# Output projection of a hybrid decoder layer: three pairs of row blocks by Strassen's algorithm

## The chip, the cores and the metric

The kernel runs on one core of a Trainium2 chip. The metric is device time in microseconds (us) of one launch. PE is the matrix engine, DVE the vector engine, ACT the scalar engine, POOL the GpSimd engine; SP is the engine that only issues transfers (the sync queue). ACT issues transfers too (its own queue), between its instructions.

## The reference

One decoder layer over 512 tokens of width 1024, in fp32. Cut to what matters here:

```python
mod = silu(c) @ ada_w + ada_b                     # adaLN: 48 blocks of 128 values
sh1, sc1, g1, sh2, sc2, g2 = split(mod, 6)
...
h = mlstm(...)                                    # 4 heads x 256 = 1024 columns
y = silu(layer_norm(causal_dwconv(a * sigmoid(gt)))) # 1024 columns
mix = concatenate([h, y]) @ w_out                 # (512 x 2048) @ (2048 x 1024)
x = x + g1 * rms_norm(mix, mix_post_g)
u = rms_norm(x, ffn_pre_g) * (1.0 + sc2) + sh2
up = causal_dwconv(u @ ffn_up)                    # then gated, ffn_down, second residual
```

## The kernel before

Every fp32 product is made of three passes: both operands are split into a high part that the matrix engine takes exactly (`hi`, a copy on ACT) and a low part (`lo`, a subtraction), and `mm3` adds hi x hi, hi x lo and lo x hi into one PSUM bank. Weights are split by `w_split`: the high part on ACT, the low part on POOL. The split blocks live in a ring of 20 tiles, ten blocks of 128 rows x 512 columns (`wpool`); raw weights come in 1 MB pieces through two buffers (`raws`) on the sync queue.

The output projection multiplies 16 row blocks of `w_out` (128 rows each: 0 to 7 from the four heads, 8 to 15 from the convolution) by the tokens, in four tiles of 128 tokens. It makes the first half of the 1024 columns (`mixa`, four PSUM banks) and then the second (`mixb`, four banks). `MIX` is the order of the blocks: those of the last head (6, 7) come late, since this head's attention is still running. `mix_first(n)` is the n-th block of the first half; calls of it stand between the steps of the last head's attention, so that PE always has something to do. The attention ends with eight transposes (`hT`); ten blocks of the first half stand ahead of them on PE, six behind. Then follow eight blocks of the second half (`KA = 8`), over all four banks. The last eight blocks are done one token tile at a time (`mix_last`), so that the norm, the residual and the modulation of a token tile (`chain_sums`, `chain_x`, `chain_u`) run beside the next tile's matmuls.

Between `KA` blocks and `mix_last` PE transposes the rows of gains for the FFN (`send_rows(KT, 2 * KT)`, tile `gT`), which go to DRAM and come back spread over all partitions (`gs2r`, `sh2r`). These gains need adaLN blocks 24 to 39. An adaLN block (`ada_block`, L147 to L157) fetches 512 KB on ACT's queue and sums it on DVE in one instruction with two inputs in SBUF; it is ordered on DVE behind the instruction that it is given. The sixteen blocks stand behind the last head's attention, and have six buffers, four of them in a tile `spare`. ACT's queue also fetches the residual `x` (eight pieces of 256 KB) and the spread row `g1r`.

The orders of PE and of the sync queue are the program's. A scheduler orders ACT, DVE and POOL by priority (program order, with `tc.cur_priority` and added dependencies as exceptions) and by when it expects operands. The FFN's down projection already works by Strassen's algorithm in Winograd's form (`forms`, `prod1`, `prod2`).

Of the kernel before, what the change touches and what calls it, by code (L numbers as in the profile page):

```python
# [22 lines left out]
H = 4  # L23
# [24 lines left out]

MIX = [*range(6), *range(8, 14), 6, 7, 14, 15]


@with_exitstack
def decoder_layer(ctx, tc, w_glu0, x, xT, c, adaT, vecs, w_glu, w_qko, w_v0, w_v, w_out, w_up, w_down, out):
    nc = tc.nc
# [92 lines left out]
    def ada_block(i, behind):  # L147

        if i % 6 < 4 and 24 <= i < 40:
            r = spare[0][:, 2 * (i % 6) : 2 * (i % 6) + 2, :].rearrange("p j t -> p (j t)")  # L150
        else:
            r = adas.tile([P, D], F32, tag="ada", name=f"ada_{i}")
        nc.scalar.dma_start(r, adaT[i // 2][:, (i % 2) * D : (i % 2 + 1) * D])
        junk = small.tile([P, D], BF16, tag="junk", bufs=1, name=f"junk_{i}")
        t = V.scalar_tensor_tensor(out=junk, in0=r, scalar=1.0, in1=cb, op0=ALU.mult, op1=ALU.mult, accum_out=mod[:, i : i + 1])  # L155
        tc.add_manual_dep(t.ins, behind.ins.name, mybir.DependencyInfo(mybir.DependencyClass.NoSync, mybir.DependencyReason.DATA),
                          reason="order on VectorE")  # L157
# [27 lines left out]

    def mm3(ps, a, b, start, stop):

        PE.matmul(ps, a[0], b[0], start=start, stop=False)  # L188
        PE.matmul(ps, a[0], b[1], start=False, stop=False)  # L189
        PE.matmul(ps, a[1], b[0], start=False, stop=stop)  # L190

# [249 lines left out]
    def pair(z, hi, lo):  # L441
        S.activation(hi, z, AF.Copy)
        V.tensor_tensor(out=lo, in0=z, in1=hi.bitcast(F32), op=ALU.subtract)
        return hi, lo

    def conv4(ps, i, name):
# [43 lines left out]
    def attention(h):  # L490
# [50 lines left out]
        for e in range(2):  # L541
# [4 lines left out]
            t = so[e]  # L546
            V.scalar_tensor_tensor(out=t, in0=t, scalar=1.0, in1=tp, op0=ALU.add, op1=ALU.mult)
            hi, lo = slot(f"hh{h}_{e}", F32R), slot(f"hl{h}_{e}", F32R)
            g = ghalf[:, 2 * h + e : 2 * h + e + 1]
# [89 lines left out]

    def send_rows(a, n, queue=nc.scalar):  # L640

        ps = mmbank(f"gT{a}") if a == KT else atbank(f"gT{a}")
        PE.transpose(ps[:n, :P], gains[:, a : a + n], ident)
        t = slot(f"gTs{a}")[:, :P]
        V.tensor_copy(t[:n, :], ps[:n, :P])
        for i in range(n // KT):
            queue.dma_start(rows_d[a // KT + i].rearrange("(j p) -> j p", p=P), t[i * KT : (i + 1) * KT, :])
# [38 lines left out]
    def wo_rows(hf, g):  # L686
        return w_load(w_out[hf, g], f"wo{hf}_{g}")

    mixa = [mmbank(f"mixa{tt}") for tt in range(NT)]

    def mix_first(n):
        if n % 4 == 0:
            wo[0] = wo_rows(0, n // 4)
        k = MIX[n]
        for tt, ps in enumerate(mixa):
            mm3(ps, (hy[k][0][:, tok(tt)], hy[k][1][:, tok(tt)]), wo[0][n % 4], n == 0, n == 2 * KT - 1)

# [64 lines left out]
    def norm_rows():  # L762
        yb = rms_bcast(yr[0], T, 1.0 / D, "ry", cvbank)
        for j in range(KT):
            V.tensor_tensor(out=ys[j], in0=ys[j], in1=yb, op=ALU.mult)
            S.activation(ys[j], ys[j], AF.Silu, bias=vcol("cv_ln_b", j), scale=vcol("cv_ln_g", j))
            hi, lo = slot(f"yh{j}", F32R), slot(f"yl{j}", F32R)
# [40 lines left out]
    gain(0, 16, "mix_post_g")  # L808
    wo = {}
    steps = attention(H - 1)  # L810
    next(steps)
    mix_first(0)
    next(steps)
    norm_rows()
    mix_first(1)
    mix_first(2)
    mix_first(3)
    mix_first(4)
    next(steps)
# [3 lines left out]
    next(steps)  # L823
    for n in range(7, 10):
        mix_first(n)
    for _ in steps:
# [5 lines left out]
    for n in range(10, 2 * KT):  # L832
        mix_first(n)
        if n == 10:
            send_rows(0, KT)
    mg = [slot(f"mg{tt}") for tt in range(NT)]
    x1 = [[slot(f"x1_{tt}_{hf}") for hf in range(2)] for tt in range(NT)]
    wide1 = vpool.tile([P, 2 * T + 8], F32, tag="vh", name="g1r")
    g1r = row(0, lambda n: [wide1[:, :T], wide1[:, T : 2 * T]], "g1")
    for tt in range(NT):  # L840
        for hf in range(2):
            nc.scalar.dma_start(x1[tt][hf], x[tok(tt), hf * T : (hf + 1) * T])
    for tt, ps in enumerate(mixa):
        V.tensor_tensor(out=mg[tt], in0=ps, in1=g1r[0], op=ALU.mult)
        sq_sum(ps, msq[:, 2 * tt : 2 * tt + 1], f"mixa{tt}")
    banks = [atbank(f"mixb{tt}") if tt < 2 else cvbank(f"mixb{tt}") for tt in range(NT)]
    for n_, k in enumerate(MIX[:KA]):
        if n_ % 4 == 0:
            wo = wo_rows(1, n_ // 4)
        for tt, ps in enumerate(banks):  # L850
            mm3(ps, (hy[k][0][:, tok(tt)], hy[k][1][:, tok(tt)]), wo[n_ % 4], n_ == 0, False)
    V.scalar_tensor_tensor(out=gains[:, KT : 2 * KT], in0=sc2[:, :, 0], scalar=1.0, in1=vcols("ffn_pre_g", 0, KT), op0=ALU.add, op1=ALU.mult)
    V.tensor_scalar(out=gains[:, KT : 2 * KT], in0=gains[:, KT : 2 * KT], scalar1=RD, scalar2=None, op0=ALU.mult)
    V.tensor_copy(gains[:, 2 * KT : 3 * KT], sc2[:, :, 1])
    wo = [w for g in range(KA // 4, 4) for w in wo_rows(1, g)]

    HT = T // 2
    u2h = upool.tile([P, 2, KT, HT], F32R, tag="uh", name="u2h")
# [43 lines left out]
    def mix_last(tt, a, b):  # L902
        for n_, k in enumerate(MIX[KA:]):
            if a <= n_ < b:
                mm3(banks[tt], (hy[k][0][:, tok(tt)], hy[k][1][:, tok(tt)]), wo[n_], False, n_ == 2 * KT - KA - 1)

# [27 lines left out]
    with in_order():  # L934
        for tt in range(3):
            mix_last(tt, 0, 2 * KT - KA)
        up_split(1, raw1, slots, "t")
# [11 lines left out]
        turn_tile(1)  # L949
        mix_last(3, 7, 2 * KT - KA)  # L950
        r = chain_sums(2)
# [309 lines left out]
def _layout(i):  # L1261
# [9 lines left out]
    def tiles(w, starts, per):  # L1271
# [20 lines left out]
    a0 = 4 * D + 2 * H  # L1292
    wo = f("w_out")[0]
    return {
        "w_glu0": c_(np.stack([cols(w_in, a0 + b * D + j * P) for j in range(4) for b in range(2)]).transpose(2, 1, 0, 3).reshape(KT, P, 8 * P)),
# [8 lines left out]
        "w_v": c_(np.stack([vw(w_in[:, 2 * D + h * DH : 2 * D + (h + 1) * DH]) for h in range(1, H)])),  # L1304
        "w_out": c_(wo.reshape(2 * KT, P, 2, T)[MIX].reshape(4, NT, P, 2, T).transpose(3, 0, 2, 1, 4).reshape(2, 4, P, 4 * T)),
        "w_up": tiles(f("ffn_up")[0], [b * DFF + j * P for j in range(NF) for b in range(2)], 2),
# [21 lines left out]
```

## Time and profile before

| | us |
|---|---|
| median of 3 runs | 773.85 |
| lowest, highest | 772.72, 775.44 |
| profiled execution, its own time | 772.58 |
| profiled execution, span of instructions | 770.9 |
| PE busy in the span | 757.8 |
| DVE, ACT, POOL busy in the span | 606.3, 403.9, 350.9 |

Rows in order of time read: start in us, duration in us, engine, line of the kernel, operation, out<-in, tile sizes, count, and in brackets the engine's idle time just before and what ended it. Durations of matmuls overlap (the next starts before the last ends), so the pitch is taken from starts.

### The profile page before, as it was taken

The page shows a single profiled execution, that of the slowest core. Times are in us where ns is not written, and L with a number is a line of the kernel's source. Part 1 is how long each engine was busy: PE and PEld are TensorE (multiplying, and loading weights), DVE is VectorE, ACT ScalarE, POOL GpSimd, SP SyncE. Part 2 cuts the span into 40 slices and gives each one's busy share as a digit, 9 for nine tenths or more (in the row PEclk, how much of TensorE's full clock was granted, in tenths as well). Part 3 has the DMA queues.
Part 4 walks back from the last instruction along what each step waited for, and adds up shares of the span by engine and source line. Part 5 has one row for each costly group of instructions (what it writes and reads, how often), then busy time and mean ns, then how long its engine had stood idle before and what let it go on. Part 6 is the DMA issues. An engine that isn't in the chain of part 4 may idle for free.

```text
span 770.9 us, 10631 instructions
## 1 busy us (share of the span) xinstructions
PE 757.8 (98%) x3709; PEld 637.3 (83%) x3709; DVE 606.3 (79%) x967; ACT 403.9 (52%) x761; POOL 350.9 (46%) x286
## 2 busy tenths in 40 slices
PE   7999999999999999999999999999999999999996
PEld 5788898778888888988888998888888888878885
DVE  6987999999999856747758798666555687699996
ACT  5447256677676457572343554444444444455762
POOL 1029578697797645442751456444444440000001
PEclk9999999999999999999999999999999999999998
DMA  8983214204023552425953653333233321787872
GB/s 325 341 334 137 84 55 164 82 29 164 28 82 110 166 177 96 162 111 187 379 195 114 245 187 130 130 130 109 96 117 124 131 91 60 260 277 226 302 261 109
DMA packets 36409, 125.33 MB, mean 163 GB/s; under 512 B 4194, under 2 KB 5634, under 8 KB 30468
## 3 DMA queue, kind: packets, MB, share of 16 engines
q1 hardware_dynamic: 24372, 96.17, 35.5%
q10 hardware_dynamic: 11984, 28.48, 10.6%
q8 instruction: 29, 0.48, 0.2%
q14 instruction: 24, 0.20, 0.1%
HBM read 113.22 MB, written 11.42 MB: 162 GB/s over the span
## 4 chain that ended last, share of the span: by engine, by line
PE 90%; DVE 4%; DMA 2%; ACT 2%; issue 1%; POOL 0%; SPq 0%; DVEq 0%; ACTq 0%; POOLq 0%
PE up L190 10%; PE up L189 10%; PE up L188 10%; PE qko L188 6%; PE qko L189 5%; PE qko L190 5%; PE p L1175 5%; PE glu L189 3%; PE glu L188 3%; PE glu L190 3%; PE glu L316 2%; PE mixa L190 2%; PE mixa L188 2%; PE mixa L189 2%; PE mixb L188 2%; PE mixb L190 2%
## 5 line engine op out<-in xcount | busy, mean ns | idle before, releaser
L721 DVE SCALAR_TENSOR_TENSOR cv<-gt,cvw,cv 128x489 f32<-128x489 f32 (+23 forms) x200 | 136.9, 728 | 3.3 <-ACT cv L709 2.2
L675 POOL TENSOR_TENSOR ro2r<-ro2t,mhalf 128x1 f32<-128x1 f32 x1 | 0.5, 537 | 120.5 <-DVE ro2t L673 120.5
L171 POOL TENSOR_TENSOR wup_1024l<-wup,wup_1024h 128x512 fp32r<-128x512 f32 x20 | 27.5, 1373 | 31.7 <-ACT wup_1024h L170 31.6
L717 POOL TENSOR_TENSOR cs<-cs,cs 128x510 f32<-128x510 f32 (+3 forms) x32 | 41.3, 1291 | 0.2
L171 POOL TENSOR_TENSOR wup_0l<-wup,wup_0h 128x512 fp32r<-128x512 f32 x20 | 27.3, 1367 | 29.1 <-ACT wup_0h L170 29.1
L171 POOL TENSOR_TENSOR wup_1536l<-wup,wup_1536h 128x512 fp32r<-128x512 f32 x20 | 27.0, 1349 | 28.8 <-ACT wup_1536h L170 28.8
L155 DVE SCALAR_TENSOR_TENSOR junk<-ada,cb 128x1024 bf16<-128x1024 f32 x20 | 31.1, 1554 | 7.8 <-DMA ada<-in_adaT 7.7
L189 PE MATMUL up<-u2l,wup_0h 128*128 128x512 f32 (+1 forms) x100 | 36.5, 365 | 0.2 <-DVE u2l L900 0.2
L188 PE MATMUL up<-u2h,wup_0h 128*128 128x512 f32 (+1 forms) x100 | 36.5, 365 | 0.0
L188 PE MATMUL up<-u2h,wup_1024h 128*128 128x512 f32 (+1 forms) x100 | 36.4, 364 | 0.0
L190 PE MATMUL up<-u2h,wup_0l 128*128 128x512 f32 (+1 forms) x100 | 36.4, 364 | 0.0
L188 PE MATMUL up<-u2h,wup_512h 128*128 128x512 f32 (+1 forms) x100 | 36.4, 364 | 0.0
L189 PE MATMUL up<-u2l,wup_512h 128*128 128x512 f32 (+1 forms) x100 | 36.4, 364 | 0.0
L190 PE MATMUL up<-u2h,wup_512l 128*128 128x512 f32 (+1 forms) x100 | 36.4, 364 | 0.0
L188 PE MATMUL up<-u2h,wup_1536h 128*128 128x512 f32 (+1 forms) x100 | 36.4, 364 | 0.0
L189 PE MATMUL up<-u2l,wup_1536h 128*128 128x512 f32 (+1 forms) x100 | 36.4, 364 | 0.0
L190 PE MATMUL up<-u2h,wup_1536l 128*128 128x512 f32 (+1 forms) x100 | 36.4, 364 | 0.0
L190 PE MATMUL up<-u2h,wup_1024l 128*128 128x512 f32 (+1 forms) x100 | 36.4, 364 | 0.0
L189 PE MATMUL up<-u2l,wup_1024h 128*128 128x512 f32 (+1 forms) x100 | 36.3, 363 | 0.0
L171 POOL TENSOR_TENSOR wup_512l<-wup,wup_512h 128x512 fp32r<-128x512 f32 x20 | 27.7, 1383 | 14.9 <-ACT wup_512h L170 14.9
L715 ACT ACTIVATE cs<-gt,cvw 128x511 f32<-128x511 f32 (+4 forms) x40 | 27.4, 715 | 8.1 <-POOL cs L717 3.6
L170 ACT ACTIVATE wup_1024h<-wup 128x512 fp32r<-128x512 f32 x22 | 13.9, 631 | 25.1 <-PE up L189 21.4
(1070 smaller groups left out, 2663.6 us busy)
## 6 DMA issues: line engine op xcount, KB each, us to landing
wup<-in_w_up SPq DMA_DIRECT2D x22, 1024.0 KB, 6.6
wqko<-in_w_qko SPq DMA_DIRECT2D x12, 1024.0 KB, 4.8
ada<-in_adaT ACTq DMA_DIRECT2D x20, 512.0 KB, 4.3
ada<-in_adaT SPq DMA_DIRECT2D x16, 512.0 KB, 7.4
wo<-in_w_out SPq DMA_DIRECT2D x8, 1024.0 KB, 4.8
spare<-in_adaT ACTq DMA_DIRECT2D x12, 512.0 KB, 7.6
wd<-in_w_down SPq DMA_DIRECT2D x6, 768.0 KB, 6.5
g2kept<-g2d SPq DMA_DIRECT2D x11, 384.0 KB, 7.3
```

The source lines that it names most:

```text
L155: t = V.scalar_tensor_tensor(out=junk, in0=r, scalar=1.0, in1=cb, op0=ALU.mult, op1=ALU.mult, accum_out=mod[:, i : i + 1])
L170: S.activation(hi[:, :n], src, AF.Copy)
L171: (eng or G).tensor_tensor(out=lo[:, :n], in0=src, in1=hi[:, :n].bitcast(F32), op=ALU.subtract)
L188: PE.matmul(ps, a[0], b[0], start=start, stop=False)
L189: PE.matmul(ps, a[0], b[1], start=False, stop=False)
L190: PE.matmul(ps, a[1], b[0], start=False, stop=stop)
L316: PE.matmul(banks0[i], blk(wk, i)[a], u[k][b], start=k == 0 and a == b, stop=False)
L675: G.tensor_tensor(out=r, in0=t, in1=mhalf[:, :1], op=ALU.pow)
L715: S.activation(t[:, d:], cvx[j][:, : T - d], AF.Copy, scale=w(CK - 1 - d))
L717: G.tensor_tensor(out=side[:, d:], in0=side[:, d:], in1=t[:, d:], op=ALU.add)
L721: last_tap[0] = V.scalar_tensor_tensor(out=cp[:, d:], in0=cvx[j][:, : T - d], scalar=w(CK - 1 - d), in1=cp[:, d:], op0=ALU.mult, op1=ALU.add)
L1175: PE.matmul(ps[q], x, y, start=False, stop=m == NM - 1 and i == 2, skip_group_check=True)
```

## The change

Ten row blocks (0 to 5 and 8 to 11) stay plain in both halves. The other six form three pairs: (12, 13), (14, 15) and (6, 7). For a pair, tokens are cut into two halves of 256, columns into two halves of 512 and rows into the two blocks, and the 2 x 2 x 2 product is made from seven products instead of eight, in Winograd's form, for both column halves at once. A product is two matmul groups of 128 tokens x 512 columns.

- `token_forms` makes sums and differences of token halves on DVE and splits them; `row_forms` and `row_late` make those of the weights.
- The products are summed over the three pairs in PSUM: P2 onto the first two `mixa` banks and P4 onto the other two, P1, then P6, then P7 in two `mixb` banks, P5 and P3 in the other two. ACT copies P1, P5 and the partial sums out, and DVE adds them where they belong (`mix_done` and the additions beside it). The second half's plain blocks are then added onto the `mixb` banks; `KA` is 2.
- The raw weights of the pairs (`w_os`, 3 MB) go into tiles that take the place of the first stage's activations. The first gains' transpose stands ahead of the last head's transposes.
- AdaLN blocks 24 to 27 stand behind the first pair's token forms, 28 to 31 behind the last pair's, 32 to 35 and 36 to 39 between the products. They have four buffers.
- `x`, the first gains' row and `g1r` go through the sync queue.

```diff
-MIX = [*range(6), *range(8, 14), 6, 7, 14, 15]
+MIX = [*range(6), *range(8, 12)]
+PAIRS = [(12, 13), (14, 15), (6, 7)]
...
-        if i % 6 < 4 and 24 <= i < 40:
-            r = spare[0][:, 2 * (i % 6) : 2 * (i % 6) + 2, :].rearrange("p j t -> p (j t)")
+        if i % 4 < 2 and 24 <= i < 40:
+            r = spare[0][:, i % 4, :]
...
-    KA = 8
+    KF = 10
+    KA = 2
...
+    def token_forms(za, zb, name):
+        sums, s4 = cvtile(f"os{name}"), cvtile(f"o4{name}")
+        s1, s2 = sums[:, :HT], sums[:, HT:]
+        V.tensor_tensor(out=s1, in0=za[:, HT:], in1=zb[:, HT:], op=ALU.add)
+        V.tensor_tensor(out=za[:, HT:], in0=za[:, :HT], in1=za[:, HT:], op=ALU.subtract)
+        V.tensor_tensor(out=s2, in0=s1, in1=za[:, :HT], op=ALU.subtract)
+        V.tensor_tensor(out=s4[:, :HT], in0=zb[:, :HT], in1=s2, op=ALU.subtract)
+        a, c, b = (pair(z, slot(f"oh{name}{n}", F32R), slot(f"ol{name}{n}", F32R)) for n, z in (("a", za), ("s", sums), ("b", zb)))
+        t = slot(f"o4{name}t", F32R)
+        t = pair(s4[:, :HT], t[:, :HT], t[:, HT:])
+        last_lo[0] = last_pair[0]
...
+    def row_forms(m):
+        b21, b11, b12, b22 = (wraw[m][:, b * T : (b + 1) * T] for b in range(4))
+        wf["p1", m] = w_split(b11, f"ob1_{m}")
+        t1 = cvtile(f"ot1_{m}")
+        V.tensor_tensor(out=t1, in0=b12, in1=b11, op=ALU.subtract)
+        wf["p5", m] = w_split(t1, f"ot1_{m}")
+
+    def row_late(which, m):
+        b = {"p2": 0, "p6": 1, "p7": 2, "p3": 3, "p4": 0}[which]
+        z = wraw[m][:, b * T : (b + 1) * T]
+        if which == "p4":
+            V.tensor_tensor(out=z, in0=z, in1=wraw[m][:, T : 2 * T], op=ALU.subtract)
+        elif which == "p6":
+            t3 = wraw[m][:, 2 * T : 3 * T]
+            V.tensor_tensor(out=t3, in0=wraw[m][:, 3 * T :], in1=t3, op=ALU.subtract)
+            V.tensor_tensor(out=z, in0=z, in1=t3, op=ALU.add)
+        wf[which, m] = w_split(z, f"o{which}_{m}")
+
+    def block(which, m):
+        ps = {"p1": banks[2:], "p6": banks[2:], "p7": banks[2:], "p5": banks[:2], "p3": banks[:2], "p2": mixa[:2], "p4": mixa[2:]}[which]
+        for q in range(2):
+            mm3(ps[q], tf[m][which][q], wf[which, m], m == 0 and which in ("p1", "p5"), m == 2, True)
...
     next(steps)
     norm_rows()
+    tf[0] = token_forms(ys[4], ys[5], "0")
...
+    for i in range(24, 28):
+        ada_block(i, last_lo[0])
+    tf[1] = token_forms(ys[6], ys[7], "1")
+    for n in range(7, KF):
         mix_first(n)
+    send_rows(0, KT, nc.sync, cvbank)
...
+    for m in range(3):
+        row_forms(m)
+    for m in range(3):
+        row_late("p2", m)
     for _ in steps:
         pass
-    spare.append(upool.tile([P, KT, T], F32, tag="ul", name="spare"))
-    for i in range(24, 40):
+    tf[2] = token_forms(*heads[H - 1][3], "2")
+    for i in range(28, 32):
         ada_block(i, last_lo[0])
...
+    for which in ("p1", "p5"):
+        for m in range(2):
+            block(which, m)
+    for m in range(2):
+        block("p2", m)
+    for which in ("p1", "p5"):
+        block(which, 2)
...
+    for i in range(32, 36):
+        ada_block(i, last_lo[0])
+
+    def mix_done(tt, also):
+        V.tensor_tensor(out=mixa[tt], in0=mixa[tt], in1=also, op=ALU.add)
+        V.tensor_tensor(out=mg[tt], in0=mixa[tt], in1=g1r[0], op=ALU.mult)
+        sq_sum(mixa[tt], msq[:, 2 * tt : 2 * tt + 1], f"mixa{tt}")
+
+    for which in ("p2", "p6", "p4", "p7", "p3"):
+        for m in range(3):
+            if which != "p2":
+                row_late(which, m)
+            if which != "p2" or m == 2:
+                block(which, m)
+        if which == "p2":
+            for q in range(2):
+                mix_done(q, op1[q])
+            for i in range(36, 40):
+                ada_block(i, last_lo[0])
+        elif which == "p6":
...
+                S.activation(ou[q], banks[2 + q], AF.Copy)
...
+                V.tensor_tensor(out=banks[q], in0=banks[q], in1=ou[q], op=ALU.add)
+        elif which == "p7":
...
+                S.activation(op7[q], banks[2 + q], AF.Copy)
...
+                V.tensor_tensor(out=banks[2 + q], in0=banks[2 + q], in1=op5[q], op=ALU.add)
+            for q in range(2):
+                mix_done(2 + q, op7[q])
     ada_done(24, 40)
...
-            nc.scalar.dma_start(x1[tt][hf], x[tok(tt), hf * T : (hf + 1) * T])
+            nc.sync.dma_start(x1[tt][hf], x[tok(tt), hf * T : (hf + 1) * T])
```

More of the change, by code (lines that the diff above doesn't have):

```diff
@@ L812, in decoder_layer @@
     mix_first(0)
+    more = upool.tile([P, 2, 2048], F32, tag="uh", name="wo_more")
+    both = upool.tile([P, 4, D], F32, tag="ul", name="spare")
+    spare.append(both)
+    wraw = [more[:, 0, :], more[:, 1, :], both[:, 2:, :].rearrange("p a n -> p (a n)")]
     next(steps)
     norm_rows()
[L815 to L818, printed above, removed]
+    tf[0] = token_forms(ys[4], ys[5], "0")
+    for n in range(1, 5):
+        mix_first(n)
+    for m, r in enumerate(wraw):
+        nc.sync.dma_start(r, w_os[m])
     next(steps)
@@ L839, in decoder_layer @@
-    g1r = row(0, lambda n: [wide1[:, :T], wide1[:, T : 2 * T]], "g1")
-    for tt in range(NT):
-        for hf in range(2):
-            nc.scalar.dma_start(x1[tt][hf], x[tok(tt), hf * T : (hf + 1) * T])
[L843 to L846, printed above, removed]
+    banks = [atbank(f"mixb{tt}") if tt < 2 else cvbank(f"mixb{tt}") for tt in range(NT)]
@@ L902, in mix_last @@
     def mix_last(tt, a, b):
[L903 removed]
+        for n_, k in enumerate(MIX[KA:KF]):
             if a <= n_ < b:
[L905 removed]
+                mm3(banks[tt], (hy[k][0][:, tok(tt)], hy[k][1][:, tok(tt)]), wo[n_], False, n_ == KF - KA - 1, True)
     def raw_up(i):
```

76 lines of the change are left out of this document (47 added, 29 removed).

## The prediction

> **What bounds the kernel now.** I read the page first, then who waited for whom on PE, then the order of time on each engine around the output projection.
>
> ```profile
> span 770.9 us, 10631 instructions
> PE 757.8 (98%) x3709; PEld 637.3 (83%) x3709; DVE 606.3 (79%) x967; ACT 403.9 (52%) x761; POOL 350.9 (46%) x286
> ...
> PE 90%; DVE 4%; DMA 2%; ACT 2%; issue 1%; POOL 0%; SPq 0%; DVEq 0%; ACTq 0%; POOLq 0%
> ```
>
> PE is busy 98% of the span, and the chain that ended last is PE for 90%. So the kernel is as long as its matmuls, as long as nothing makes PE wait. The list of PE's waits is short, and its last three rows are these:
>
> ```profile
> PE s L504 <- DVE E L505: 0.4, 1, 0.4
> PE p L189 <- DVE t_4l L1004: 0.3, 1, 0.3
> PE up L189 <- DVE u2l L900: 0.2, 1, 0.2
> ```
>
> No row names mixa, mixb or gT: through the output projection PE waits for nothing. A matmul taken out there is worth its full pitch, and any new wait there is paid in full, because no idle time follows on PE that could absorb it. The next view is PE in order of time, with the last transposes of the last head (hT), two points of the first half twelve matmuls apart, and the transpose of the FFN gains (gT) behind eight blocks of the second half.
>
> ```profile
> 352.44 1.03 PE L545 MATMUL hT<-ident,hn 128*128 128x128 f32 x8
> ...
> 361.64 0.39 PE L188 MATMUL mixa<-wo_512h,hh 128*128 128x512 f32 x1
> ...
> 364.36 0.39 PE L188 MATMUL mixa<-wo_1024h,yh 128*128 128x512 f32 x1
> ...
> 391.56 0.27 PE L643 MATMUL gT<-ident,gains 128*16 128x128 f32 x1
> ```
>
> Twelve matmuls take 364.36 - 361.64 = 2.72 us, a pitch of 0.227 us (the 0.39 is one matmul from end to end, pipelined). The gT transpose needs `gains`, and these need all sixteen adaLN blocks 24 to 39 on DVE. DVE in order of time:
>
> ```profile
> 359.38 1.23 DVE L155 SCALAR_TENSOR_TENSOR junk<-spare,cb 128x1024 bf16<-128x1024 f32 x1
> ...
> 360.65 1.23 DVE L155 SCALAR_TENSOR_TENSOR junk<-spare,cb 128x1024 bf16<-128x1024 f32 x1
> ...
> 389.04 1.23 DVE L853 TENSOR_SCALAR gains<-gains 128x8 f32<-128x8 f32 x1
> 391.87 0.28 DVE L645 COPY gTs<-gT 16x128 f32<-16x128 f32 x1 [1.61 <-PE gT L643]
> ```
>
> The gains are ready at 389.04 + 1.23 = 390.3; PE comes for them at 391.56. The margin is 1.3 us. This is what the prediction turns on: DVE's chain to the gains is almost as long as PE's work over the same stretch, and the stretches around it show where there is room.
>
> ```profile
> 340.00:353.00 13.00, 13.00 (x68) 11.01 (x68) 1.35 (x5) 4.67 (x15) 6.43 (x7) 1.00 0.21 82
> 353.00:390.00 37.00, 37.00 (x168) 30.57 (x167) 31.89 (x45) 11.77 (x24) 21.92 (x13) 1.00 0.82 299
> ```
>
> The columns are PE, PEld, DVE, ACT, POOL (busy us and count), clock, DMA share, GB/s. Before 353 DVE works 1.35 us of 13; after it, 31.9 of 37, beside 13 POOL instructions.
>
> **The matmuls.** Before: 16 blocks x 4 token tiles x 3 passes x 2 halves = 384. After: 10 plain blocks in each half give 240, and a pair is 7 products x 2 token tiles x 3 passes = 42, so three pairs give 126: 366 in all. Eighteen fewer, 18 x 0.227 = 4.1 us. All of them lie between hT and gT (150 matmuls against 168), so PE reaches gT at 391.56 - 4.1 = 387.5. The first gains' transpose only moves ahead of hT. DVE's chain, to gain the whole 4.1, must end 2.8 us earlier than now.
>
> **DVE's chain to the gains.** Its present parts, grouped over 353 to 390 (busy, mean ns, idle ahead of them):
>
> ```profile
> L155 DVE SCALAR_TENSOR_TENSOR junk<-spare,cb 128x1024 bf16<-128x1024 f32 x12 | 18.0, 1497 | 4.2 <-DMA spare<-in_adaT 4.0
> L155 DVE SCALAR_TENSOR_TENSOR junk<-ada,cb 128x1024 bf16<-128x1024 f32 x4 | 5.4, 1350 | 0.6 <-DMA ada<-in_adaT 0.5
> L844 DVE TENSOR_TENSOR mg<-mixa,g1r 128x512 f32<-128x512 f32 x4 | 2.5, 675 | 0.0
> L551 DVE SCALAR_TENSOR_TENSOR hl<-so,ghalf,hh 128x512 fp32r<-128x512 f32 x2 | 1.4, 749 | 0.2 <-ACT hh L550 0.2
> L547 DVE SCALAR_TENSOR_TENSOR so<-so,hT 128x512 f32<-128x512 f32 x2 | 1.3, 683 | 5.1 <-PE hT L545 5.1
> ```
>
> The additions are subtractions and sums of 512 or 256 columns; their nearest rows are a 512-wide one from SBUF and, from the FFN's own Strassen forms, a 256-wide one (min/median/max in ns):
>
> ```profile
> 401.32 1.28 DVE L879 TENSOR_TENSOR un<-x,gs2r 128x512 f32<-128x512 f32 x2
> L1013 DVE TENSOR_TENSOR ysum<-ysum,F x11: 412/418/420, 458.9 to 666.6; 128x256 f32<-128x256 f32 x11
> ```
>
> So 0.64 and 0.42 us. What leaves the chain: four adaLN blocks go into DVE's empty time ahead of 353, 4 x 1.27 (360.65 - 359.38) = -5.1; hl of the last head -1.4; two of the four mg products fall behind the sixth and seventh products, -1.2. The waits for adaLN data, 4.0 + 0.5 = 4.5, come while x (2 MB) and the adaLN weights share ACT's queue; x goes to the sync queue and four blocks are fetched earlier, so I take -4.5, bounds 0 and -4.5. What comes in: the token forms of the last pair stand ahead of block 28 by an explicit order on DVE, four half-wide operations and low parts of three full and one half tile, 4 x 0.42 + 3 x 0.64 + 0.42 = +4.0. Row forms for P6 (six operations) and P4 (three), 9 x 0.64 = +5.8, of which I let three of P6's use the room before 353, -1.9 (bounds 0 and -3.8: all six need only that P1's and P5's forms have been read from the raw weights). Adding P1 to two banks and U2 to two banks, four at the PSUM rate of mg (2.5 / 4 = 0.62), +2.5. Sum: -5.1 - 1.4 - 1.2 - 4.5 + 4.0 + 5.8 - 1.9 + 2.5 = -1.8 us. That is not yet the 2.8 wanted, and the weight splits still have to come in.
>
> **The splits on POOL.** Each prepared weight block costs one ACT copy and one POOL subtraction. Before there are 32, after 20 + 21 = 41. The ring holds ten blocks, so the same 19 are done by 353 in both; 22 are left against 13. POOL, then DVE, in the same stretch of time:
>
> ```profile
> 377.18 2.27 POOL L171 TENSOR_TENSOR wo_1024l<-wo,wo_1024h 128x512 fp32r<-128x512 f32 x1
> 379.41 2.27 POOL L171 TENSOR_TENSOR wo_1536l<-wo,wo_1536h 128x512 fp32r<-128x512 f32 x1
> ...
> 387.69 1.28 POOL L171 TENSOR_TENSOR wo_1024l<-wo,wo_1024h 128x512 fp32r<-128x512 f32 x1
> 388.94 1.30 POOL L171 TENSOR_TENSOR wo_1536l<-wo,wo_1536h 128x512 fp32r<-128x512 f32 x1
> 376.56 1.74 DVE L155 SCALAR_TENSOR_TENSOR junk<-ada,cb 128x1024 bf16<-128x1024 f32 x1 [0.48 <-DMA ada<-in_adaT]
> ```
>
> Alone, splits follow each other at 388.94 - 387.69 = 1.25 us and adaLN blocks at 1.27. Together, a split and a block take 379.41 - 377.18 = 2.2 us: they take turns, and each split costs DVE about 1.0 us. The mg products, which read PSUM, show no such stretch. Nine more splits therefore cost the chain 9 x 1.0 = +9.0. Bounds: 0, if POOL does them while DVE reads PSUM or waits (a gain is excluded: more splits cannot speed DVE up), and +15, if all 22 collide where now the 13 collide in part (the adaLN blocks' 23.4 us are 3.7 above 16 x 1.23, and the three gains operations about 1 each above what 8 or 16 columns need, like the 1.23 of L853). I take 9.0, nearer to the middle, since DVE has fewer gaps than now.
>
> The Trainium skill ("SBUF — State Buffer", section on who interferes with whom) calls this an exclusive lock: a DVE instruction with two SBUF inputs and a GpSimd instruction that reads SBUF block each other fully. By that rule a split would cost its whole 1.25, 11.3 in place of 9.0, an estimate 2.3 us later; the measured pitch of 2.2 is a little under the 2.52 of both in full, so the row is used.
>
> **The sum.** The gains are ready at 390.3 - 1.8 + 9.0 = 397.5, PE comes at 387.5: it waits 10.0 us, and 10.0 - 4.1 = +5.9. Whether DVE's lateness shows at gT, or earlier at a P6 block or a bank that waits for its addition, changes the place and not the price, since all wait for the same queue. A wait that long also has a price on PE's clock (the columns as above):
>
> ```profile
> 764.00:768.00 4.00, 0.39 (x2) 0.00 (x0) 2.92 (x5) 1.38 (x4) 0.54 (x1) 0.87 0.31 114
> 768.00:770.90 2.90, 0.00 (x0) 0.00 (x0) 0.00 (x0) 0.00 (x0) 0.00 (x0) 0.50 0.47 177
> ```
>
> After the last matmuls (0.39 us in that row) the granted clock falls to 0.50; a mean of 0.87 over 764 to 768 means that it fell at about 767, 2.6 us after PE stopped at 764.4. How long the half clock lasts when matmuls resume, no row shows; bounds are 0 and a few us; I take the time of the fall, at half speed a loss of 1.3 us. The Trainium skill ("TensorE: Matmul & The Clock Gate", Part 1) says that about 3.4 us of work lift it again: by that, an estimate of 1.7 us lost, 0.4 more.
>
> With 1.3 the change costs 5.9 + 1.3 = 7.2. The profiled execution took 772.58 us (span 770.9 and 1.7 around it), which gives 779.8. The median of the runs shown is 1.3 above the profiled one, so the prediction is 781.0.
>
> **What costs nothing, and its cover.** A split's copy on ACT, and the first POOL split behind a long idle time of both:
>
> ```profile
> 368.19 0.63 ACT L170 ACTIVATE wo_512h<-wo 128x512 fp32r<-128x512 f32 x1 [11.48 <-DMA x<-in_x]
> 368.89 1.30 POOL L171 TENSOR_TENSOR wo_512l<-wo,wo_512h 128x512 fp32r<-128x512 f32 x1 [10.63 <-ACT wo_512h L170]
> ```
>
> ACT gains nine copies for splits, eight out of PSUM and four for the last pair's forms, 21 x 0.63 = 13 us beside 11.8 of 37: it has room, and between P1 and the P6 that overwrites its bank lie two blocks of PE work, 2.7 us; without them PE would wait for two copies. The x loads on the sync queue stand behind the second half's weights, and are wanted only after 400. The first gains' rows on the sync queue hold back those weights until hT; they are used 126 matmuls, 28 us, later. The last pair's forms have six blocks, 36 x 0.227 = 8.2 us, as cover against 4.0 on DVE, 1.3 for the two products ahead of them and some ACT copies.
>
> **The rivals.** *In time* (faster): POOL's extra splits fall beside DVE's PSUM work and gaps, cost nothing, and P6's forms all fit before 353. The chain ends at 390.3 - 1.8 - 1.9 = 386.6, PE finds its gains, and the 4.1 are kept: 769.8. It decides at 387.5. For it speaks the idle time in the two rows above: ACT stood 11.5 us behind transfers that it had to issue, POOL got no split, and the adaLN blocks ran at 1.27. Against it: the new order of work uses weights twice as fast, so POOL must not stand still. *Held splits* (slower still): the same stop of ACT recurs, behind adaLN buffers that DVE frees late (four now, six before). PE has nine blocks in hand, 9 x 6 x 0.227 = 12.2 us, until 365.4; with the first new split done at 368.89 + 1.3 = 370.2 and eleven more at 2.2, the last comes at 394.4, and gT after 1.4 + 24 x 0.227 at 401.2: 9.6 later than now, 783.5. *Half the port's price*: the extra splits cost what the present 13 do on average, (3.7 + 3) / 13 = 0.5 each: the chain ends at 393.1, PE waits 5.6, +1.5, or +2.8 with the clock: 775.4 to 776.7. *Not what it says*: a product that was not shorter for PE than the rows it replaces; the FFN's own products are 128x512 matmuls like the plain rows, so I give it nothing.
>
> **How the numbers follow.** About 0.3% (2.3 us) is what a measurement of this kernel can tell from no change. Forecast 0.50, in time 0.25, held splits 0.15, half price 0.10. The half price splits into 0.07 within 0.3% and 0.03 slower; so faster 0.25, same 0.07, slower 0.68. The forecast's own range is 775 to 788: down by waits and forms that find room, up when all 22 splits collide (+6) or the waits for data stay (+4.5). Both signs hold weight, so the range goes from 769.5, the rival in time, to 787, with the rest of the high bounds outside.
>
> **What would show it.** Right: a new row in PE's waits of about 10 us, gT behind the gains operations on DVE, or blocks waiting for DVE forms or POOL splits; adaLN blocks of some 2 us and splits of 2.2 us between 360 and 395; clock under 1.00 just after the wait; 18 fewer matmuls on PE. Wrong: gT at about 387.5 without a wait and a span of about 767.

## The result

| | us | against the kernel before |
|---|---|---|
| before, median of 6 runs | 773.07 (772.42 to 775.44) | |
| after, median of 6 runs | 795.21 (791.35 to 797.74) | ratio 1.0281, 95% interval 1.0250 to 1.0311 |
| after, profiled execution | 797.74 (span 795.8) | span +24.9 |

The change costs 22 us. The direction was forecast, the size was not: 795.2 lies 14 us above the predicted 781.0 and 8 us above the range. The page of the kernel after, in the lines that answer to those of before:

```profile
span 795.8 us, 10707 instructions
...
PE 761.9 (96%) x3691; PEld 638.6 (80%) x3691; DVE 644.7 (81%) x1005; ACT 415.9 (52%) x786; POOL 372.9 (47%) x295
...
PEclk9999999999999999996999999999999999999999
```

The 18 matmuls are gone (3691 against 3709), DVE has 38 us more to do, and in one slice of the span the clock is down. PE's waits between 300 and 425 us, where before there was only one of 0.2:

```profile
PE hT L547 <- DVE hn L541: 11.5, 2, 10.8
PE gT L648 <- DVE gains L948: 3.0, 1, 3.0
PE mixb L190 <- ACT op L904: 2.0, 1, 2.0
PE mixb L190 <- DVE mixb L939: 1.8, 2, 1.4
```

That is 18.3 us, and only 3.0 of them at gT, where the prediction put 10.0. The largest wait is at the last head's transposes (hT). DVE in order of time ahead of them, in the kernel before and then after:

```profile
344.62 0.20 DVE L533 TENSOR_TENSOR dm<-dm,em 128x4 f32<-128x4 f32 x1 [4.80 <-ACT dm L526]
346.87 1.14 DVE L539 TENSOR_SCALAR hn<-hn,fac 128x256 f32<-128x256 f32 x4 [2.04 <-POOL fac L536]
```

```profile
345.36 1.21 DVE L156 SCALAR_TENSOR_TENSOR junk<-spare,cb 128x1024 bf16<-128x1024 f32 x1
...
346.50 1.79 DVE L735 TENSOR_TENSOR wo_more<-wo_more 128x512 f32<-128x512 f32 x1
...
355.68 2.32 DVE L156 SCALAR_TENSOR_TENSOR junk<-ada,cb 128x1024 bf16<-128x1024 f32 x1
...
362.80 0.15 DVE L535 TENSOR_TENSOR dm<-dm,em 128x4 f32<-128x4 f32 x1
...
366.20 3.14 DVE L541 TENSOR_SCALAR hn<-hn,fac 128x256 f32<-128x256 f32 x4 [0.30 <-POOL fac L538]
```

From 345.36 to 362.80 DVE works without a gap: adaLN blocks, forms for P5 and P6, low parts of the second pair. A form of 512 columns takes 1.8 us here and 0.68 alone. All of it stands ahead of `dm` and `hn`. ACT is late too, because its own queue is in order:

```profile
354.58 0.64 ACT L171 ACTIVATE ot_2h<-ot 128x512 fp32r<-128x512 f32 x1 [1.82 <-DVE ot L725]
...
355.42 0.15 ACT L528 ACTIVATE dm<-o 128x1 f32<-128x1 f32 x1
```

The last `dm` copy of the head stands behind the copies of weight forms, which wait for DVE. Its operand had long been there: PE's last `o` product (348.32, 0.28 long) ends at 348.60, ACT copies `dm` 6.8 us later, and DVE multiplies it 7.2 us after the copy. In the kernel before both followed within 0.3 us. What the slow forms stand beside is seen on POOL, and why POOL is so late on the sync queue:

```profile
337.64 1.29 POOL L172 TENSOR_TENSOR wo_0l<-wo,wo_0h 128x512 fp32r<-128x512 f32 x1 [14.50 <-ACT wo_0h L171]
...
347.70 1.75 POOL L172 TENSOR_TENSOR ob_1l<-wo_more,ob_1h 128x512 fp32r<-128x512 f32 x1
```

```profile
320.23 0.80 SPq L871 DMA_DIRECT2D wo_more<-in_w_os  x2
...
321.60 0.53 SPq L179 DMA_DIRECT2D wo<-in_w_out  x1
```

The load of the last two plain blocks (`wo`) stands behind the pairs' weights, whose tiles are free only at 320. POOL idles 14.5 us, and these blocks' splits and those after them fall beside DVE's forms. PE in order of time at three of the waits:

```profile
367.70 0.45 PE L547 MATMUL hT<-ident,hn 128*128 128x128 f32 x1 [10.77 <-DVE hn L541]
...
371.38 0.63 PE L190 MATMUL mixb<-ob_0h,ol0a 128*128 128x512 f32 x1
371.80 0.63 PE L190 MATMUL mixb<-ob_0h,oh0a 128*128 128x512 f32 x1
...
387.31 0.50 PE L190 MATMUL mixb<-op_0h,oh0s 128*128 128x512 f32 x1 [2.01 <-ACT op L904]
...
390.98 0.47 PE L190 MATMUL mixb<-op_2h,oh2s 128*128 128x512 f32 x1
...
415.69 0.37 PE L648 MATMUL gT<-ident,gains 128*16 128x128 f32 x1 [3.03 <-DVE gains L948]
415.71 0.77 PE L190 MATMUL mixb<-wo_0h,hh 128*128 128x512 f32 x1
...
418.42 0.41 PE L190 MATMUL mixb<-wo_1024h,hh 128*128 128x512 f32 x1
```

After these three waits the matmuls come 0.43 us apart (371.80 - 371.38) instead of 0.227; after the fourth row's two, of 0.4 and 1.4, they do not. From 387.31 to 390.98 there are nine, 3.67 us in place of 2.04: 1.6 lost behind a wait of 2.0. From 415.71 to 418.42 there are six, 1.35 lost. After hT it is about 2.9: eight matmuls (370.38 to 373.94) lose 1.7, and the eight transposes take 1.95 without their own wait of 0.7 where they took 0.79 before. Together 5.9 us.

The span's +24.9 is so: waits 18.3, half clock 5.9, matmuls -4.1, and 4.2 in the opening, where this execution had waits of its own, as these stretches of after show (columns as in the prediction; before, PE was busy 34.18 and 259.65 us at a clock of 1.00):

```profile
0.00:40.00 40.00, 32.26 (x129) 25.05 (x130) 30.47 (x78) 18.84 (x33) 4.16 (x12) 0.96 0.91 320
40.00:300.00 260.00, 258.93 (x1287) 217.29 (x1286) 230.57 (x368) 155.57 (x301) 182.82 (x146) 1.00 0.35 123
340.00:353.00 13.00, 13.00 (x71) 11.24 (x70) 13.00 (x16) 7.33 (x22) 7.53 (x6) 1.00 0.18 53
353.00:390.00 37.00, 23.49 (x90) 18.46 (x89) 33.75 (x40) 15.30 (x30) 24.37 (x18) 0.78 0.34 113
```

The opening's part is 1.9 + 0.7 of PE's time and 40 x 0.04 of clock; it differs between executions (PE was busy 33.99 us of the first 40 in run 16 below, which keeps one pair, and 32.09 in run 4, the kernel before but for `x`), so it is hardly the change's, and may be why the profiled execution is 2.5 us above the median. Some 0.6 us are not placed.

### The profile page after: what moved, and what is told of

Its sections match the earlier page's. It is cut to its first block, busy times and chain, and to the rows that moved or that the text cites. A ratio compares the mean times of both kernels' runs of the same rounds, so it can differ in the third digit from the quotient of the medians.

```text
span 795.8 us, 10707 instructions
## 1 busy us (share of the span) xinstructions
PE 761.9 (96%) x3691; PEld 638.6 (80%) x3691; DVE 644.7 (81%) x1005; ACT 415.9 (52%) x786; POOL 372.9 (47%) x295
## 5 line engine op out<-in xcount | busy, mean ns | idle before, releaser
L156 DVE SCALAR_TENSOR_TENSOR junk<-ada,cb 128x1024 bf16<-128x1024 f32 x24 | 39.7, 1655 | 7.3 <-DMA ada<-in_adaT 6.9
L172 POOL TENSOR_TENSOR wup_512l<-wup,wup_512h 128x512 fp32r<-128x512 f32 x20 | 27.7, 1386 | 14.5 <-ACT wup_512h L171 14.5
L171 ACT ACTIVATE wup_1024h<-wup 128x512 fp32r<-128x512 f32 x22 | 13.9, 630 | 25.0 <-PE up L190 21.4
```

What stands on the lines that cost most here:

```text
L171: S.activation(hi[:, :n], src, AF.Copy)
L172: (eng or G).tensor_tensor(out=lo[:, :n], in0=src, in1=hi[:, :n].bitcast(F32), op=ALU.subtract)
```

## The experiments

All times are medians; "lost" is against the kernel before in the same series (773.1 to 775.4). "Waits" are PE's between 300 and 425 us (in runs 7 and 8 from 290, in run 13 to 440). All runs but the fourth change the kernel after.

| run | time | ratio, 95% interval | lost | waits |
|---|---|---|---|---|
| after | 795.2 | 1.0250 to 1.0311 | 22.1 | 18.3 |
| 1 `hn` first on DVE | 798.7 | 1.0297 to 1.0339 | 24.6 | 19.6 |
| 2 adaLN 24 to 39 left out | 780.3 | 1.0057 to 1.0090 | 6.2 | 7.7 |
| 3 both | 784.6 | 1.0107 to 1.0164 | 10.5 | 10.3 |
| 4 before, x on the sync queue | 782.7 | 1.0089 to 1.0126 | 8.6 | 6.3 |
| 5 plain rows' load first | 789.4 | 1.0171 to 1.0217 | 14.0 | 15.4 |
| 6 that, and order on DVE | 790.7 | 1.0183 to 1.0230 | 15.3 | 13.4 |
| 7 that, and adaLN 24 to 31 early | 787.2 | 1.0139 to 1.0183 | 11.8 | 11.0 |
| 8 adaLN 24 to 31 early alone | 793.0 | 1.0206 to 1.0261 | 17.6 | 15.2 |
| 9 as 6, behind `so` | 789.6 | 1.0179 to 1.0220 | 16.1 | 12.9 |
| 10 as 9, adaLN left out | 774.2 | 0.9993 to 1.0018 | 0.7 | 2.8 |
| 11 as 9, nine splits left out | 782.0 | 1.0091 to 1.0130 | 8.2 | 7.2 |
| 12 as 9, two pairs | 784.1 | 1.0112 to 1.0156 | 10.6 | 8.2 |
| 13 as 12, adaLN by the sync queue | 793.1 | 1.0210 to 1.0268 | 19.6 | 13.9 |
| 14 as 12, plain rows spread | 785.5 | 1.0135 to 1.0184 | 11.8 | 10.3 |
| 15 as 14, one pair | 789.0 | 1.0179 to 1.0213 | 15.3 | 11.6 |
| 16 as 15, adaLN behind `hn` | 775.4 | 1.0015 to 1.0034 | 1.8 | 2.4 |

The last two columns rise and fall together: what is lost is PE's waiting and the half clock behind it. The theory at the start was that DVE's new work stands ahead of `hn` (placement, A or A2 in the expectations); its rival, that DVE and POOL have too much to do, so that any order only moves the wait (volume, B). Where the expectations name e6_wo_first or e7_order_fix, runs 5 and 6 are meant, and where that of run 12 speaks of a first kernel, run 9.

**Runs 1 to 3: order against volume.**

```diff
+            tc.add_manual_dep(t.ins, last_hn[0].ins.name, ..., reason="order on VectorE")
...
     for i in range(24, 28):
-        ada_block(i, last_lo[0])
+        ada_block(i, last_hn[0])
```

(the dependency is put on the forms and low parts of the changed part), and for runs 2 and 3

```diff
     def ada_block(i, behind):
+        if 24 <= i < 40:
+            return
```

> The changed kernel, with one thing added: on DVE the second pair's token forms, the row forms and adaLN blocks 24 to 27 are ordered behind the last head's four scalings (hn). In the changed kernel PE waits 11.5 us for hn at the transposes hT, 3.8 us among the products and 3.0 at gT. Theory A (order: the new work was put ahead of the denominators and hn on DVE): the wait at hT falls under 1 us, the half clock behind it goes too (some 2.5 us), the other waits grow by less than 4: 782 to 786 us. Rival B (volume: DVE has too much work before the gains, wherever it stands): what is saved at hT comes back at the products or at gT: 791 us or more.

> The changed kernel without adaLN blocks 24 to 39 (neither fetched nor summed; those gains are then the bias alone). Theory A: of the DVE work ahead of hn only the blocks 24 to 27 go, 1.2 to 2.3 us each, so hT still waits some 5 us; the waits at gT and for the banks go: 780 to 785 us. Rival B (volume): 16 blocks of 1.3 to 2.3 us are more than the whole of the waits (18.3), so all waits go and the 18 matmuls are gained: 768 to 771 us.

> Both edits: DVE order behind hn, and adaLN blocks 24 to 39 left out. Theories A and B both give no wait over 1 us and the full gain of the matmuls, 768 to 771 us. Rival C (the weight splits on POOL, 22 against 13, taking turns with DVE, cannot follow PE at one block in 1.36 us): waits of 3 us or more stay at products whose weights are not split: 774 us or more.

PE's waits in run 1, the two largest:

```profile
PE mixb L190 <- DVE gTs L658: 8.0, 1, 8.0
PE mixb L190 <- ACT op L913: 5.7, 2, 5.1
```

The wait at hT is gone and 19.6 us stand elsewhere: the copy of the first gains (`gTs`), whose bank `mixb` takes next, came behind the work that was held. The time is what volume expected (791 or more); that no other order helps it does not show, since the late `gTs` is itself a matter of place. Run 2 gains 14.9 us on the kernel after, with one wait left, 7.7 at hT: that is what placement expected (780 to 785), while volume's 768 to 771 was a miss. Run 3 missed both: all theories but C had no wait there, and C's would have been for split weights, not the 5.1 at `gTs` and 5.2 at the last pair's operands that it has. The 16 adaLN operations are untouched work of before; without them most of the loss is gone, so the amount of work counts, and the 7.7 that stay at hT say that its place counts too.

**Run 4: x on the sync queue, in the kernel before.**

```diff
-            nc.scalar.dma_start(x1[tt][hf], x[tok(tt), hf * T : (hf + 1) * T])
+            nc.sync.dma_start(x1[tt][hf], x[tok(tt), hf * T : (hf + 1) * T])
```

> The kernel before, with only the residual x moved from ACT's queue to the sync queue: one part of the change alone. All theories: no wait of PE is there to be removed, so within 0.3% of the kernel before, 772 to 775 us; ACT's stop of 11.5 us ahead of 368 gets shorter. If it is slower by more, the queue order itself is part of the loss.

The sync queue and PE's largest wait:

```profile
345.72 17.90 SPq L842 DMA_DIRECT2D x<-in_x  x8
363.71 28.85 SPq L178 DMA_DIRECT2D wo<-in_w_out  x4
```

```profile
PE mixb L188 <- ACT wo_0h L170: 3.9, 1, 3.9
```

In the order of the kernel before x stands ahead of the second half's weights on this queue, in the kernel after behind them. The 772 to 775 expected were a miss. But the order differs, so the run tells nothing of the change's own move; it shows that a queue that only issues is still a queue.

**Runs 5 to 8: the load first, the order whole, adaLN earlier.**

```diff
-        if n % 4 == 0:
-            wo[0] = wo_rows(0, n, min(n + 4, KF))
+        if n in (0, 4):
+            wo[n] = wo_rows(0, n, n + 4)
+        if n == 4:
+            wo[8] = wo_rows(0, 8, KF)
```

Run 6 adds: the second pair's token forms, the forms for P1 and P5 and the first gains' transpose earlier in the program, and P6's forms and adaLN 24 to 27 ordered behind `hn`. Runs 7 and 8 put adaLN 24 to 31 behind the last tap of the convolution, ahead of the last attention.

> The changed kernel, with the load of the plain rows 9 and 10 (the last two of the first half) issued on the sync queue ahead of the three pair loads, which wait there until the first stage's activations are free. In the changed kernel POOL stands still for 14.5 us (322 to 337.6) for want of those weights and then splits in the very stretch in which DVE has the new forms. Theory A2 (place: the new DVE work stands ahead of hn and takes turns with POOL there): two or three splits leave the stretch, about 1 us each, hT's wait falls from 11.5 to 8 or 9 us: 790 to 793 us. Rival B (volume of DVE work before the gains): nothing is taken away, 794 to 797 us.

> The changed kernel, nothing taken away, four things moved: the plain rows' load as in e6_wo_first; the second pair's token forms and the row forms T1 emitted before the last head's scalings; P6's forms and adaLN blocks 24 to 27 ordered behind hn on DVE; the first gains' transpose and its copy ahead of the middle of the first half. Theory A2 (place): the wait at hT is under 3 us, some waits at the products and at gT stay, 776 to 784 us. Rival B (volume): as much is lost at the products and at gT as hT gains, 789 us or more.

> e7_order_fix, and adaLN blocks 24 to 31 moved to before the last head's attention (behind the convolution's taps, where DVE has some 14 us of idle time between 276 and 316). The same work in all. If both place and the stretch's volume count: hT under 3 us, nothing at gT, 769 to 774 us, the first that could keep the matmuls' 4 us. If the splits on POOL (22 behind hT) are a limit of their own: waits for weights at the products, 776 us or more.

> The changed kernel with only the adaLN blocks 24 to 31 moved ahead of the last head's attention. Theory A2 (place): hT still waits for hn behind the forms, as without any adaLN block (7.7 us there), the waits at products and gT mostly go: 780 to 785 us. Rival B (volume): 8 blocks of 1.3 to 2.3 us leave the stretch, 10 to 18 us: 777 us or less if it were the sum alone.

Run 5 brings the time from 795.2 to 789.4, 6 us (8 by the loss), about what placement expected (790 to 793, hT 8 or 9; it is 9.2): POOL does three splits ahead of its idle time that had come behind it. The idle time itself stays:

```profile
339.74 2.10 POOL L172 TENSOR_TENSOR ot_0l<-ot,ot_0h 128x512 fp32r<-128x512 f32 x1 [15.43 <-ACT ot_0h L171]
```

The split behind it needs a form that DVE and ACT have not made yet. In run 6 the wait at hT is gone, and PE waits 5.8 for `so`, behind P6's forms and adaLN blocks on DVE, and 4.5 for the gains; 790.7 is what volume expected. Runs 7 and 8 gain 3.5 us on run 6 and 2 on the kernel after, and pay with a new wait at 292 and 297 (3.4 and 4.5, PE for ACT's `hn` copies): ACT's queue stood behind transfers for adaLN that had no free buffer. Run 7 lies where the splits on POOL were expected to set the limit (776 or more), but none of its waits is for split weights; run 8 lies outside both expectations.

**Runs 9 to 11: volume, and which.** Run 9 orders the same work behind `so`. Run 10 leaves adaLN out of it, run 11 keeps it and drops nine subtractions on POOL:

```diff
-        wf[which, m] = w_split(z, f"o{which}_{m}")
+        wf[which, m] = w_split(z, f"o{which}_{m}", two=which not in ("p6", "p4", "p7"))
```

> The order of the earlier orderings with one step more: VectorE's P6 forms and adaLN 24 to 27 now also stand behind the last head's `so`, whose lateness held the banks for 5.8 us when they stood only behind `hn`. Theory (VectorE and GpSimd have too much to do between 345 and 415, and order only chooses where PE waits): the 5.8 us at `so` go, and most of them turn up again at the second half's first banks, the operand copies and the second gains' transposition; 786 to 791 us against 790.7 of that ordering. Rival (the loss is all placement): what was waited for at `so` is gone for good, waits add to under 8 us; 780 to 784 us.

> The same with adaLN blocks 24 to 39 left out (16 operations of 1.21 us on VectorE; the second branch's scale and shift are then wrong inputs of the same size). Theory (volume): with the room that they free and this order, no wait over 1 us stays between 330 and 420, and the 18 matmuls saved show: 768 to 772 us, that is 2 to 5 us below the kernel before. Rival (the six row blocks' own chain, forms on VectorE and operand copies on ScalarE, can't keep up whatever else there is to do): waits of 4 us and more stay at the operand copies or the second half's banks, 775 to 782 us.

> The three pairs in the order that waits least so far (forms and adaLN behind the last head's `so`, 789.6 us), with the low part of the weights of P6, P4 and P7 left out: the high part is multiplied in its place, so PE's matmuls, VectorE's work and ScalarE's copies are the same and only nine subtractions on GpSimd go. Theory (GpSimd's splits make VectorE late by taking turns, about 1.0 us each): 9 us less waiting in all and a half-clock stretch fewer, 777 to 781 us. Rival (VectorE's own added operations make it late, the splits lie beside them): 786 to 790 us.

PE's waits in run 9 and in run 11, the two largest from 300 on:

```profile
PE mixb L190 <- DVE ol2a L443: 7.1, 1, 7.1
PE mixb L190 <- DVE mixb L947: 3.4, 2, 3.0
```

```profile
PE mixb L193 <- DVE mixb L950: 2.6, 2, 1.4
PE mixb L193 <- DVE ol2a L446: 2.6, 1, 2.6
```

And the stretch from 365 to 390, of run 9 and then of run 11:

```profile
365.00:390.00 25.00, 17.47 (x60) 13.64 (x61) 24.97 (x29) 11.94 (x22) 18.57 (x12) 0.73 0.39 129
```

```profile
365.00:390.00 25.00, 22.20 (x89) 17.55 (x89) 24.93 (x34) 14.27 (x27) 17.37 (x9) 0.93 0.65 208
```

DVE works all 25 us in both, 29 instructions in one and 34 in the other. In run 9 the wait at `so` came back further on, at the last pair's low parts, as volume had it. Nine splits less give 5.7 us less waiting (12.9 to 7.2) and 7.6 us of time, a little short of the 9 expected and well away from the rival's 0 to 4: a split on POOL costs 0.63 us of PE's waiting, and with the clock 0.84. (Nine tiles of the split ring are free as well; what that adds was not taken apart.) Run 10 has no wait in the projection at all, as volume had it, but it does not beat the kernel before. Its waits:

```profile
PE xT L1001 <- DVE u2l L1009: 1.2, 1, 1.2
PE xT L1001 <- DVE un L993: 1.0, 1, 1.0
PE xT L1001 <- DVE un L978: 0.6, 1, 0.6
```

PE now comes earlier than DVE's chain of norm, residual and modulation, and 2.8 of the 4.1 us are waited away there; what took the other 1.3 is not placed. The 768 to 772 us expected were a miss by 2. Leaving adaLN out also takes sixteen transfers off ACT's queue. That DVE's time counts here, and not that queue, is argued from run 9's full 25 us on DVE; it was not tried apart.

**Runs 12 to 16: fewer pairs, to find one that pays.** Two pairs (12 matmuls saved), then one (6); the last head's blocks 6 and 7 go back to plain rows.

```diff
-MIX = [*range(6), *range(8, 12)]
-PAIRS = [(12, 13), (14, 15), (6, 7)]
+MIX = [*range(6), *range(8, 12), 6, 7]
+PAIRS = [(12, 13), (14, 15)]
```

Run 13 issues adaLN's loads on the sync queue; run 14 puts half of rows 6 and 7 between P6 and P4. Run 16 differs from run 15 by this alone:

```diff
+    for i in range(24, 32):
+        ada_block(i, last_hn[0])
...
-    for i in range(24, 28):
-        ada_block(i, last_so[0])
-    for i in range(28, 32):
-        ada_block(i, last_lo[0])
```

> Two pairs instead of three: the last head's rows 6 and 7 are multiplied plainly, behind the transposes (6 more products of 18 matmuls saved are given back: 12 saved, 2.7 us). VectorE loses the third pair's token forms and row forms (8 + 4 operations) and regains two low parts; GpSimd splits 38 row tiles, not 41. The order is that of the run with the work behind `so`, and adaLN has four buffers of the spare tile. Theory (volume): waits fall from over 10 to 3 to 8 us; 775 to 782 us. Rival (placement only): no change against the three pairs in the same order but for the 1.4 us of matmuls, so as the first kernel of this call plus 1.4.

> The same two pairs with the loads of adaLN 24 to 39 issued by the sync queue instead of ScalarE. If ScalarE's operand copies stand behind those issues (each of which waits for a buffer that VectorE frees), the waits of PE at the operand copies go: 1 to 3 us less than with ScalarE's queue, 773 to 780 us. If it is VectorE's volume alone, no change within 1 us, or worse by up to 2, because the second half's weights then stand behind them on the sync queue.

> Two pairs in that order (784.1 us, of which 2.7 us of waiting on ScalarE's copies of P6's banks), with the last head's rows 6 and 7 split by token tiles: those of tiles 0 and 1 stand ahead of P2's last block, those of tiles 2 and 3 between P6 and P4, so that 12 matmuls (2.7 us) cover the copies. Theory (VectorE's and GpSimd's volume): the wait on ScalarE goes, and about half of it comes back at the second gains' transposition; 781 to 784 us. Rival (placement): it stays gone, with its half clock; 779 to 781 us.

> One pair (rows 14 and 15) in the same order: 6 matmuls saved (1.4 us), one extra set of forms (4 operations for tokens, 4 for rows, the additions to the banks), 35 splits. Theory (volume): three pairs cost about +16 us and two +11 in this order, so one costs +4 to +6 with waits of 3 to 5 us; 777 to 780 us. Rival (there is a margin of 1 to 3 us on VectorE that one pair fits into): no wait over 1 us, 771.5 to 774 us, level with the kernel before or up to 1.4 below it.

> One pair as before (789.0 us, 9.4 us waited for the second gains), with adaLN 24 to 31 ordered behind the last head's `hn` instead of behind `so`: VectorE stood idle 10.5 us between the two, which takes eight operations of 1.21 us. Theory (VectorE's hours between 345 and 400 decide): the wait for the gains falls from 9.4 to under 2 us, its half clock with it, and the time to 774 to 778 us; at best level with the kernel before, as the gain to be had is 1.4 us. Rival (one pair's own chain of copies and additions is too long whatever the order): gains still 4 us and more late, 780 to 785 us.

Two pairs in the order of run 9 cost 10.6 us, with 8.2 of waits, 2 us above what volume expected and 7 below its rival. Run 13 is a miss: the second half's weights on the sync queue then stand behind adaLN's transfers, and PE waits 7.7 for their split. Run 14 is a miss too: the wait for ACT's copies goes, and 5.6 in one piece come back at the additions on DVE. Run 15 fell outside both expectations. DVE's waits in it show why:

```profile
DVE so L555 <- PE hT L553: 10.5, 1, 10.5
DVE junk L156 <- ACT mixa1junk L676: 6.6, 1, 6.6
```

The order that helped three pairs left DVE idle for one: adaLN was held behind `so`, which waits for PE's transposes. Run 16 puts eight blocks into that time. DVE and PE's waits:

```profile
347.94 1.14 DVE L547 TENSOR_SCALAR hn<-hn,fac 128x256 f32<-128x256 f32 x4 [2.02 <-POOL fac L544]
349.00 1.22 DVE L156 SCALAR_TENSOR_TENSOR junk<-spare,cb 128x1024 bf16<-128x1024 f32 x1
...
357.86 1.22 DVE L156 SCALAR_TENSOR_TENSOR junk<-spare,cb 128x1024 bf16<-128x1024 f32 x1
...
387.53 1.23 DVE L954 TENSOR_SCALAR gains<-gains 128x8 f32<-128x8 f32 x1
```

```profile
PE xT L996 <- DVE u2l L1004: 1.2, 1, 1.2
PE mixb L190 <- DVE mixb L945: 0.8, 2, 0.6
```

(A third, of 0.4, follows.) The gains are ready at 388.8, no wait is left at gT, and 13.7 us come back by one order (789.0 to 775.4). So placement and volume are both needed: with one pair, where there is room, order decides these 13.7 us; with two and three pairs none of the orders tried found the room. Even here the ratio is 1.0025 (1.0015 to 1.0034): the 1.4 us saved are less than the 2.4 that PE waits. No version beats the kernel before.

## Why the prediction was wrong, by its own steps

- **The matmuls, -4.1: right** as a count (18 fewer). That a matmul taken out is worth its full pitch did not hold: even with adaLN left out (run 10), 2.8 of it was waited away at xT.
- **"Four adaLN blocks go into DVE's empty time ahead of 353", -5.1, and three of P6's forms, -1.9: the step that failed.** By the prediction's own prices the room was overfull: 13 - 1.35 = 11.65 us were empty, the two terms take 7.0, and P5's three forms (3 x 0.64 = 1.9) and the second pair's token forms (4.0, as for the last pair), needed just behind hT, stand in no term of the sum: 12.9 in all. Nor was the room free. It was empty because DVE had nothing to do between waiting for ACT's `dm` (4.80 us) and for PE's hT (5.07 us), and the prediction let the instructions after these waits stay in place. Nothing kept them there: the scheduler put 17.4 us of work ahead of `dm` (adaLN 4.5, forms for P6 6.3, for P5 3.4, low parts of the second pair 3.2), and PE paid 11.5 at hT. The prediction had costed the first two as a gain and the others at nothing.
- **"Whether DVE's lateness shows at gT, or earlier ... changes the place and not the price": wrong.** The gains were ready at 415.5 and not at 397.5, but PE came for them only at 412.7. The waits earlier on, 15.3 us, did not take the place of the forecast 10.0; of those 3.0 stayed. And the place had a price: the same work waits 12.9 us in the order of run 9 and 19.6 in that of run 1.
- **The splits, +9.0: right in kind, too large.** Run 11 has 5.7 us of waiting for nine. The row (1.0 each) was nearer than the exclusive lock of the Trainium skill ("SBUF — State Buffer", section on who interferes with whom), by which it would be 11.3. That part of the splits lay beside PSUM work, as the lower bound allowed, would fit and was not shown.
- **The clock, +1.3: right in size for two waits, wrong in number.** 1.35, 1.6 and 2.9 us after three waits, 5.9 in all. The first two are near the 1.7 worked out from the Trainium skill ("TensorE: Matmul & The Clock Gate", Part 1); the third, after the longest wait, is 1.2 above it.
- **Waits on ACT costed at nothing: wrong.** With 52% busy it had room, but its queue is in order: PE waited 2.0 for `op`, and ACT's `dm` copy, behind forms that DVE had not made, came 6.8 us after its operand.
- **The rivals.** *Held splits* happened, at another place and from another cause: POOL stood still 14.5 us ahead of hT, for a load on the sync queue and not for adaLN buffers, and the new splits came all the later; run 5 prices that load's place at 6 to 8 us. *In time* and *half the port's price* needed the -5.1 to be real. *Not what it says* is out: the count of matmuls fell as written.

The sum on the right terms: waits 18.3 + clock 5.9 - 4.1 = 20.1, of the 22.1 measured between medians; 2 us are not placed.

## What to carry to other kernels

Idle time in front of an instruction that waits for an operand is not free room: work put there must end before the operand comes, and something in the program must hold it to that order; one such order was worth 13.7 us in the version with one pair. A saving on PE is to be weighed against what it adds to the engines that feed PE in the same stretch: 18 matmuls, 4.1 us, were bought with 38 us more of busy time on DVE and 22 on POOL, the turns that the two take with each other included. When a wait is ordered away, look where it comes out again, and leave work out once: if the wait vanishes only then, the engine is full.

## What the runs showed of the hardware that was not expected

- PE's clock can fall behind a short wait, and the length of the wait alone does not decide it. After 2.01 us of idle time nine matmuls took 3.67 us instead of 2.04 (rows of after above). After 2.51 us in run 7 they came 0.23 us apart from the second on:

```profile
365.21 0.50 PE L190 MATMUL mixb<-ot_0h,oh0s 128*128 128x512 f32 x1 [2.51 <-DVE so L555]
365.54 0.39 PE L190 MATMUL mixb<-ot_0l,oh0s 128*128 128x512 f32 x1
365.77 0.39 PE L190 MATMUL mixb<-ot_0h,ol0s 128*128 128x512 f32 x1
```

In run 11 two waits of 1.2 and 1.4 us, with three matmuls between them (394.33 to 396.67), were enough: from 397.55 on the matmuls are 0.43 us apart. In runs 10 and 16, whose longest waits were 1.2 us, the granted clock is 1.00 in every stretch from 300 to 420. What decides in between was not tried.
- The last head's `hn`, four operations of 128x256 with one tensor and a column of factors, took 3.14 us beside POOL's splits (in the kernel after two of these start at 366.14 and 367.36) and 1.14 in run 16, where POOL has no split from 346 to 364. So DVE takes turns with POOL not only where it reads two tensors.
- The last `gains` operation, 8 columns wide, took 1.23 us before (L853 in the prediction's rows) and 0.17 in the kernel after (L948):

```profile
415.37 0.17 DVE L948 TENSOR_SCALAR gains<-gains 128x8 f32<-128x8 f32 x1
```

The 1.23 was not the operation's own time. It ran from 389.04 to 390.27, beside the split on POOL from 388.94 to 390.24 in the prediction's rows; in run 16 it again takes 1.23, from 387.53, beside a split from 387.43 to 388.73; in the kernel after POOL's last split had ended at 415.11.
